# The first loads of a hybrid decoder layer: their order, pieces and buffers

## The chip, the core and the metric

The kernel runs on one core of one Trainium2 chip. The metric is the device time of one execution in microseconds, as the median of several runs. All tensors are float32 in memory; the large products run as split products, in which each operand is cut into a high part (a float32r copy) and a low part (what the copy leaves over).

## The reference, cut to what matters

One decoder layer with 256 tokens and a model width of 2048. A normalised input goes through one combined projection, from which three kinds of token mixers read: six retention heads, six mLSTM heads and 32 groups of an S5 state-space model. Their outputs pass an output projection, and a convolutional gated MLP of width 5632 follows.

```
h = rmsnorm(x, norm1_w)
proj = h @ w_in                      # r_q, r_k, r_v, r_g, m_qk, m_v, m_o, m_gates, s_u
x = x + concat(ret_out, mlstm_out, s5_out) @ w_out
h = rmsnorm(x, norm2_w)
x = x + (silu(gate) * val) @ w_down  # val, gate = split(causal_dwconv(h @ w_up))
return rmsnorm(x, final_norm_w)
```

The change concerns only the beginning: the loads of x, of the parameters and of the 512 columns of `w_in` that make `s_u`, the input of the S5 groups (called the u projection here).

## The kernel before

**Products.** A weight tile `wr` (or `s` for the early pairs, from pool `p4`) is loaded from memory, ScalarE copies it to a float32r tile `wh` (line 412, `highs_to`), and VectorE subtracts to get the low part `wl` (line 423, `lows_to`). The activations are split in the same way into tiles of 512 columns: 256 high, 256 low. A high weight times the whole activation tile and a low weight times the high activation give the product. Matmul, VectorE, ScalarE and GpSimd instructions are all issued through helpers, so the profile shows them on lines 236, 184, 194 and 203, and 219.

**The stream of weights.** All weights form one list, `items`, in the order of their use. `loads_to(i)` (line 381) issues the DMAs up to item i, `highs_to` the casts, `lows_to` the subtractions. The u projection is items 0 to 9: the first four (`NS = 4`) hold one K tile of 128 rows with its 512 columns, 256 KB each, and go to `wr` buffers. Items 4 to 9 hold two K tiles each, 512 KB ("pairs"), and go to six of the eight buffers of pool `p4`, one buffer each, so that no load of a pair waits for a buffer. Later items go through four `wr` buffers.

**The front.** ScalarE's queue issues item 0's DMA and then that of the small parameters `pp0` (lines 1174 and 1175). SP's queue issues everything else: line 1202 loops over j = 0 to 9 and issues the x tile or tiles for item j (`load_x`, 128 KB for a K tile) and then item j. TensorE runs nine matmuls on constants meanwhile.

**The loop of the u projection** (line 1255) goes over the ten items. For each it scales the x tiles by the norm's weight into the high part (ScalarE, for K tile 0 VectorE), subtracts for the low part (VectorE, `scalar_tensor_tensor`), calls `lows_to(j)`, inserts a few small VectorE instructions of the S5 parameters (`fill`), calls `loads_to(j + 4)` (line 1273), squares a tile of x for the norm from j = 4 on, and issues the matmuls: for each K tile four with the high weights, then four with the low ones, into the PSUM tiles `acc` (two) and `u` (two). So K tiles 4 and 5 are item 4, tiles 6 and 7 item 5, and so on.

**Order of the work.** Up to the MLP the schedule is written by hand: the program keeps modelled clocks of the engines and of the DMA (`clk`), and `pump()` places pending tasks (evacuations, S5, heads) between the matmul tiles by these clocks. Each engine then runs its instructions in the order in which they were issued. The small loads in `later` (identity, rotary table, S5 matrices) are issued one behind each weight load.

Of the kernel before, what the change touches and what calls it, by code (L numbers as in the profile page):

```python
# [33 lines left out]
NP0 = _PP["n2"][0]  # L34
# [6 lines left out]
def kernel(ctx: ExitStack, tc: tile.TileContext, a: dict, out: bass.AP):  # L41
    nc = tc.nc
    ADD, SUB, MUL, MAX = ALU.add, ALU.subtract, ALU.mult, ALU.max
# [66 lines left out]
    def free(ap):  # L110
        return int(np.prod(ap.shape[1:]))
# [31 lines left out]
    def landed(ap, at):  # L143
        key, lo, hi = span(ap)
        wrote.setdefault(key, []).append((lo, hi, "dma", at))
# [6 lines left out]
    def reuse(tag, ap, bufs):  # L152

        key = ap.tensor.name
        old = slots.setdefault(tag, [])
        if len(old) >= bufs:
            first = min(old, key=last)
            old.remove(first)
            was_read[key] = [(0, 1 << 30) + x[2:] for tab in (wrote, was_read) for x in tab.get(first, ())]
        old.append(key)  # L160
        return ap
# [68 lines left out]
    V, S, G = Vec(), Act(), Pool()  # L230
# [31 lines left out]
    def add(gen, hi=False):  # L262
        (hi_tasks if hi else lo_tasks).append([gen, ("dve", 0.0)])
# [46 lines left out]
    pp0 = const.tile([128, NP0], F32, name="pp0")  # L310
# [23 lines left out]
    NS = 4  # L334
    items += [([a["wu"][:, 512 * i:512 * (i + 1)]], 512) for i in range(NS)]
    add_stream(a["wu"][:, NS * 512:], (KT - NS) * 512)
    NU = len(items)
# [31 lines left out]
    raw, high, split, ready = {}, {}, {}, {}  # L369
# [4 lines left out]
    auto = [False]  # L374

    later, loaded = [], set()

    def have(*tiles):
        return "obj", lambda: all(t.tensor.name in loaded for t in tiles)

    def loads_to(i):
        while nxt[0] <= min(i, len(items) - 1):
            j = nxt[0]
            ap, n = items[j]
            if NS <= j < NU:

                t = s4()
            else:
                t = reuse("wr", wraw.tile([128, CH], F32, tag="wr", name=f"wr{j}"), 4)
            for i, z in enumerate(ap):  # L390
                (nc.sync if j else nc.scalar).dma_start(out=t[:, i * n // len(ap):(i + 1) * n // len(ap)], in_=z)
            if not auto[0]:
                free_at = max([x[3] for x in was_read.get(t.tensor.name, ())], default=0.0)
                clk.dma = max(clk.dma, free_at + 1.3) + n / 703.0
                landed(t, clk.dma + 0.91)
            if later:

                dst, src = later.pop(0)
                nc.sync.dma_start(out=dst, in_=src)
                clk.dma += free(dst) / 703.0  # L400
                landed(dst, clk.dma + 0.91)
                loaded.add(dst.tensor.name)
            raw[j] = t
            nxt[0] += 1

    def highs_to(i):
        while nxt[1] <= min(i, len(items) - 1):
            j = nxt[1]
            loads_to(j)
            n = items[j][1]  # L410
            h = reuse("wh", whi.tile([128, CH], F32R, tag="wh", name=f"wh{j}"), 4)
            S.copy(h[:, :n], raw[j][:, :n])
            high[j] = h
            nxt[1] += 1

    def lows_to(i):
        while nxt[2] <= min(i, len(items) - 1):
            j = nxt[2]
            highs_to(j)
            n = items[j][1]  # L420
            t, h = raw.pop(j), high.pop(j)
            l = reuse("wl", wlo.tile([128, CH], F32R, tag="wl", name=f"wl{j}"), 3)
            V.tensor_tensor(l[:, :n], t[:, :n], h[:, :n], op=SUB)
            split[j] = (h, l)
            ready[j] = clk.dve + 0.26
            nxt[2] += 1
# [323 lines left out]
    def s4():  # L750
        return p4.tile([128, 1024], F32, tag="s4", name=name("s4"))
# [216 lines left out]
    def ret_heads():  # L968
        yield "obj", lambda: len(rqk) == 6 and (1, 1) in rv
        dec, o_sb, sd = [], {}, {}  # L970
        for h in range(6):
            d = s2()
            later.append((d[:, :384], a["decay"][h]))
            dec.append(d)
        yield have(*dec)

        def scores(hp):
            yield "pe", clk.dve
            yield from grab("mis", 2)
            pss = [mis_t(), mis_t()]  # L980
            for lo, hi, kc, q0 in ((0, 256, 0, 0), (256, 384, 1, 128)):
                for e in range(2):
                    r = slice(64 * e, 64 * e + 64)
                    mm(pss[e][:, lo:hi], lhsT=rqk[3 + hp][r, kc * 128:(kc + 1) * 128], rhs=rqk[hp][r, q0:],
                       start=True, stop=True, par=2)
            yield "dve", clk.pe + 0.2
            for e in range(2):
                d = dec[2 * hp + e]
                V.tensor_tensor(d[:, :384], d[:, :384], pss[e][:, :384], op=MUL)
                sd[2 * hp + e] = d  # L990
            room["mis"] += 2

        yield from scores(0)
        yield from scores(1)
        for half in range(2):
            if half:
                yield from scores(2)
            yield "pe", clk.dve + 0.2
            yield from grab("mis", 2)
            po = [mis_t(), mis_t()]  # L1000
            for i in range(3):
                h = half * 3 + i
                w = slice(i * 128, (i + 1) * 128)
                mm(po[0][:, w], lhsT=sd[h][:, 0:128], rhs=rv[0, half][:, w], start=True, stop=True)
                mm(po[1][:, w], lhsT=sd[h][:, 128:256], rhs=rv[0, half][:, w], start=True, stop=False)
                mm(po[1][:, w], lhsT=sd[h][:, 256:384], rhs=rv[1, half][:, w], start=False, stop=True)
            yield "dve", clk.pe
            for t in range(2):
                o = s2()
                S.copy(o[:, :384], po[t][:, :384])  # L1010
                o_sb[t, half] = o
            room["mis"] += 2
        yield "dve", clk.act + 0.1
        yield from head_norm(o_sb, rg, P("rgn"), 0)
# [156 lines left out]
    manual.enter_context(tc.manual_schedule())  # L1171


    loads_to(0)
    nc.scalar.dma_start(out=pp0, in_=a["pp"][:, :NP0])
    nc.gpsimd.memset(onesm, 1.0)

    nc.scalar.activation(tn([128, 1]), onesm[:, 0:1], AF.Square)
# [11 lines left out]
    def load_x(k, n):  # L1190
        c = k // 2
        if xr[c] is None:
            xr[c] = s2()
        w = slice((k % 2) * T, (k % 2 + n) * T)
        nc.sync.dma_start(out=xr[c][:, w], in_=a["x"][c][:, w])
        clk.dma += 0.37 * n
        for i in range(n):
            xat[k + i] = clk.dma + 0.91
        landed(xr[c][:, w], clk.dma + 0.91)

    kts = [[j] if j < NS else [2 * j - NS, 2 * j - NS + 1] for j in range(NU)]
    for j in range(NU):
        load_x(kts[j][0], len(kts[j]))
        loads_to(j)
    add(ret_heads())
    add(gates())
    add(ml_heads())
# [47 lines left out]
    for j, ks in enumerate(kts):  # L1255
        pump(until=max(last(raw[j].tensor.name), xat[ks[-1]]))
        for k in ks:
            d, x = s2(F32R), xr[k // 2][:, (k % 2) * T:(k % 2 + 1) * T]
            if k == 0:
                V.tensor_scalar(d[:, :T], x, P("n1", k), None, op0=MUL)  # L1260
            else:
                S.activation(d[:, :T], x, AF.Copy, scale=P("n1", k))
            xs.append(d)
        fill(j == 0)

        n = 2 if 0 < j < NS else 1
        for k in ks:
            V.scalar_tensor_tensor(xs[k][:, T:], xr[k // 2][:, (k % 2) * T:(k % 2 + 1) * T], P("n1", k),
                                   xs[k][:, :T], op0=MUL, op1=SUB)
            fill(n)  # L1270
        lows_to(j)
        fill(n + (j == 0))
        loads_to(j + 4)
        if j + 4 == NU:
            rot = s2()
            raws = [s2() for _ in range(4)]
            later += [(ident, a["ident"]), (rot, a["rot"])]
            later += [(raws[i], a["s5b" if i < 2 else "s5c"][i % 2]) for i in range(4)]
            later += [(pp1, a["pp"][:, NP0:])]
            st["raws"] = raws  # L1280
        if j >= NU - 6 and len(sqs) < 8:
            square()
            fill(1)
        hl = split.pop(j)
        for i, k in enumerate(ks):
            o = [slice(i * 512 + f * 128, i * 512 + (f + 1) * 128) for f in range(4)]
            for f in range(4):
                mm(ups[f], lhsT=hl[0][:, o[f]], rhs=xs[k], start=(k == 0), stop=False)
            for f in range(4):
                mm(ups[f][:, T:], lhsT=hl[1][:, o[f]], rhs=xs[k][:, :T], start=False, stop=(k == KT - 1))  # L1290
# [179 lines left out]
    for i in range(NFF):  # L1470
# [6 lines left out]
        j, k = 2 * i, 2 * i + 1  # L1477
# [11 lines left out]
    for f in range(14):  # L1489
        t = fm_sum(fm_tile(st_dn[f], gact, NFF))  # L1490
# [186 lines left out]
```

## Time and profile before

| | us |
|---|---|
| median of 3 runs | 1141.56 |
| lowest and highest of them | 1141.35, 1142.52 |
| the profiled execution | 1142.12 |
| its span | 1140.0 |

In the profile, PE is TensorE's matmuls and PEld its weight loads, DVE is VectorE, ACT ScalarE, POOL GpSimd, and SP the engine that only issues DMAs; a "q" behind the name is the engine's queue when it issues. A row of a timeline gives start, duration, engine, line, operation and tiles (out<-in), and in brackets the idle time before it and what ended it. A row of a DMA view gives the count of issues, the size of one and the median microseconds from issue to landing. A row of the waits gives the total, the number of waits and the longest. In a row of stages the figures are the busy time of PE, PEld, DVE, ACT and POOL, TensorE's granted clock, the DMA's share and GB/s.

### The profile page before, as it was taken

What the parts mean: (1) busy time and instruction counts of PE and PEld (TensorE: products, weight loads), DVE (VectorE), ACT (ScalarE), POOL (GpSimd) and SP (SyncE); (2) the same over time, 40 slices, a digit from 0 to 9 for tenths busy, and PEclk for the clock granted to TensorE, in tenths of its full rate; (3) what the DMA queues carried; (4) which work ended last, traced back from release to release, by engine and by line L of the source; (5) the groups of instructions that cost most, each with busy time, mean ns of one, the idle gap of its engine ahead of it and who ended that gap; (6) DMA issues with size and microseconds to landing.
All of it is one profiled execution on the core that took longest, in us unless ns stands there. A gap on an engine that the chain in (4) does not pass through costs nothing.

```text
span 1140.0 us, 18148 instructions
## 1 busy us (share of the span) xinstructions
PE 1128.1 (99%) x6660; PEld 1009.4 (89%) x6660; DVE 875.5 (77%) x1532; ACT 629.6 (55%) x996; POOL 84.8 (7%) x170
## 2 busy tenths in 40 slices
PE   9999999999999999999999999999999999999997
PEld 8899888998988888888888888888888888888897
DVE  8899989998989977777777777777777545544454
ACT  7665567345656765555555555555555444444442
POOL 7506050022000000000000000000000000000000
PEclk9999999999999999999999999999999999999999
DMA  8657555555676655555556555555655566666663
GB/s 317 213 168 242 171 162 160 153 159 151 189 244 210 201 186 185 188 191 192 191 191 192 184 187 187 191 191 190 193 191 188 177 197 183 188 187 192 194 189 108
DMA packets 68933, 215.87 MB, mean 189 GB/s; under 512 B 7782, under 2 KB 11116, under 8 KB 68844
## 3 DMA queue, kind: packets, MB, share of 16 engines
q1 hardware_dynamic: 68556, 214.41, 59.4%
q8 instruction: 52, 0.85, 0.3%
q14 instruction: 37, 0.30, 0.1%
q10 hardware_dynamic: 288, 0.31, 0.1%
HBM read 212.58 MB, written 2.10 MB: 188 GB/s over the span
## 4 chain that ended last, share of the span: by engine, by line
PE 95%; DVE 1%; ACT 1%; POOL 1%; DMA 1%; issue 0%; SPq 0%; DVEq 0%; ACTq 0%; POOLq 0%
PE acc L236 90%; PE mis L236 3%; PE wo L236 1%; POOL t L219 1%; DVE s L184 1%; ACT s L203 1%; PE u L236 1%; DMA s<-in_wu_dram 1%; DVE wl L184 1%; PE mis L240 0%; ACT wh L194 0%; DMA wr<-in_wu_dram 0%; DVE t L184 0%; ACT L203 0%; POOL tp L219 0%
## 5 line engine op out<-in xcount | busy, mean ns | idle before, releaser
L194 ACT CAST wh<-wr 128x1024 fp32r<-128x1024 f32 (+3 forms) x411 | 408.0, 995 | 417.7 <-PE acc L236 263.3
L236 PE MATMUL acc<-s,wh 128*128 128x512 f32 x2372 | 579.2, 392 | 1.0 <-ACT wh L194 0.6
L184 DVE TENSOR_TENSOR wl<-wr,wh 128x1024 fp32r<-128x1024 f32 (+3 forms) x411 | 462.8, 1150 | 148.1 <-PE acc L236 94.9
L236 PEld LDWEIGHTS acc<-s,wh 128*128 128x128 f32 x2372 | 432.6, 188 | 82.8 <-ACT wh L194 0.8
L236 PEld LDWEIGHTS acc<-s,wl 128*128 128x128 f32 x2372 | 310.7, 191 | 16.2 <-DVE wl L184 0.5
L236 PE MATMUL acc<-s,wl 128*128 128x256 f32 x2372 | 317.9, 283 | 0.1
L184 DVE TENSOR_TENSOR s<-s,s 128x256 f32<-128x256 f32 (+5 forms) x271 | 127.4, 487 | 45.5 <-ACT s L203 41.8
L236 PE MATMUL acc<-wh,s 128*128 128x384 f32 (+2 forms) x632 | 157.6, 329 | 0.0
L184 DVE SCALAR_TENSOR_TENSOR s<-s,pp,s 128x255 f32<-128x255 f32 (+3 forms) x244 | 116.7, 479 | 8.5 <-ACT s L203 5.3
L236 PEld LDWEIGHTS acc<-wh,s 128*128 128x128 f32 x632 | 112.1, 189 | 2.3 <-issue 1.5
L236 PE MATMUL acc<-wl,s 128*128 128x384 f32 (+2 forms) x316 | 103.3, 327 | 1.0 <-DVE wl L184 1.0
L203 ACT ACTIVATE s<-s,pp 128x256 f32<-128x256 f32 (+1 forms) x145 | 81.8, 568 | 15.4 <-DVE s L184 14.6
L184 DVE TENSOR_TENSOR s<-acc,s 128x256 f32<-128x256 f32 x138 | 57.6, 421 | 38.9 <-ACT s L194 35.8
L219 POOL TENSOR_TENSOR t<-t,neg_half 128x2 f32<-128x2 f32 (+1 forms) x4 | 2.5, 635 | 870.0 <-DVE t L184 870.0
L236 PEld LDWEIGHTS acc<-wl,s 128*128 128x128 f32 x316 | 59.6, 189 | 2.0 <-DVE wl L184 1.9
L203 ACT ACTIVATE s<-s 128x256 f32<-128x256 f32 (+2 forms) x105 | 45.0, 429 | 28.8 <-DVE s L184 28.7
L194 ACT COPY s<-acc 128x256 f32<-128x256 f32 (+1 forms) x142 | 52.0, 369 | 3.0 <-PE acc L236 2.8
L236 PE MATMUL acc<-g,wh 128*128 128x512 f32 x196 | 49.5, 392 | 0.0
L184 DVE TENSOR_TENSOR s<-s,rbc 128x256 f32<-128x256 f32 x106 | 44.7, 425 | 6.1 <-ACT rbc L194 3.1
L236 PEld LDWEIGHTS acc<-g,wh 128*128 128x128 f32 x196 | 35.8, 188 | 6.9
L236 PE MATMUL mis<-s,s 128*32 128x256 f32 (+6 forms) x216 | 25.8, 340 | 0.6 <-DVE s L184 0.6
L236 PEld LDWEIGHTS acc<-g,wl 128*128 128x128 f32 x196 | 25.4, 191 | 1.1
(105 smaller groups left out, 471.0 us busy)
## 6 DMA issues: line engine op xcount, KB each, us to landing
wr<-in_wup_dram SPq DMA_DIRECT2D x176, 512.0 KB, 4.8
wr<-in_wdn_dram SPq DMA_DIRECT2D x70, 512.0 KB, 4.2
wr<-in_wtm_dram SPq DMA_DIRECT2D x56, 384.0 KB, 3.3
wr<-in_wfm_dram SPq DMA_DIRECT2D x36, 512.0 KB, 5.0
wr<-in_wout_dram SPq DMA_DIRECT2D x16, 512.0 KB, 4.5
wr<-in_wdt_dram SPq DMA_DIRECT2D x11, 512.0 KB, 3.7
wr<-in_wout_dram SPq DMA_DIRECT2D x20, 256.0 KB, 4.2
s<-in_x_dram SPq DMA_DIRECT2D x14, 256.0 KB, 6.8
```

Of the source, the lines that this page charges most:

```text
L184: return real(o, *args, **kw)
L194: return nc.scalar.copy(o, i)
L203: return nc.scalar.activation(o, i, fn, **kw)
L219: return real(o, *args, **kw)
L236: nc.tensor.matmul(o, lhsT=lhsT, rhs=rhs, start=start, stop=stop)
```

## The change

- The parameters' DMA is issued before that of item 0, both still on ScalarE's queue.
- The cast of item 0 and both the cast and the subtraction of item 4 (the first pair) are made in two halves of its columns. Item 0's subtraction stays whole.
- Item 4 is loaded in two DMAs of one K tile each, and its two x tiles one by one, in the order x, weights, x, weights.
- The pairs use three `p4` buffers in turn instead of six. Before the loop only items 0 to 6 are issued; pair j + 3 (with its x tiles) is issued in the loop after `lows_to(j)`. The later items are issued from j = 7 on with `loads_to(j + 4)`.

```diff
@@ loads_to
             if NS <= j < NU:
-                t = s4()
+                if len(early_w) < 3:
+                    early_w.append(s4())
+                t = early_w[(j - NS) % 3]
             else:
                 t = reuse("wr", wraw.tile([128, CH], F32, tag="wr", name=f"wr{j}"), 4)
+            if j == NS:
+                ap = [ap[0][:, :512], ap[0][:, 512:]]
             for i, z in enumerate(ap):
+                if j == NS:
+                    load_x(kts[j][i], 1)
                 (nc.sync if j else nc.scalar).dma_start(out=t[:, i * n // len(ap):(i + 1) * n // len(ap)], in_=z)
@@
+    def halves(j, n):
+        return (slice(0, n // 2), slice(n // 2, n)) if j in (0, NS) else (slice(0, n),)
@@ highs_to
-            S.copy(h[:, :n], raw[j][:, :n])
+            for w in halves(j, n):
+                S.copy(h[:, w], raw[j][:, w])
@@ lows_to
-            V.tensor_tensor(l[:, :n], t[:, :n], h[:, :n], op=SUB)
+            for w in halves(j, n) if j else (slice(0, n),):
+                V.tensor_tensor(l[:, w], t[:, w], h[:, w], op=SUB)
@@ the front
+    nc.scalar.dma_start(out=pp0, in_=a["pp"][:, :NP0])
     loads_to(0)
-    nc.scalar.dma_start(out=pp0, in_=a["pp"][:, :NP0])
@@
-    for j in range(NU):
-        load_x(kts[j][0], len(kts[j]))
+    def load(j):
+        if j < NU and j != NS:
+            load_x(kts[j][0], len(kts[j]))
         loads_to(j)
+    for j in range(NS + 3):
+        load(j)
@@ the loop
-        loads_to(j + 4)
+        if NS <= j < NU - 3:
+            load(j + 3)
+        elif j >= NU - 3:
+            loads_to(j + 4)
```

More of the change, by code (lines that the diff above doesn't have):

```diff
@@ L376 @@
     later, loaded = [], set()
+    early_w = []
     def have(*tiles):
```

## The prediction

> **What bounds the kernel now.** I read the page's busy shares first, then the chain of waits over the first 60 us, then the engines' timelines there, and last who keeps TensorE waiting after 30 us.
>
> ```profile
> span 1140.0 us, 18148 instructions
> PE 1128.1 (99%) x6660; PEld 1009.4 (89%) x6660; DVE 875.5 (77%) x1532; ACT 629.6 (55%) x996; POOL 84.8 (7%) x170
> ```
>
> TensorE is busy for 1128.1 of 1140.0 us. No edit touches a matmul, so all that this change can move is a part of the 11.9 us in which TensorE stands, or runs behind its data. The chain of waits (start, us, what) shows which part lies in the front:
>
> ```profile
> 0.71 3.25 DMA wr<-in_wu_dram
> ...
> 4.83 6.62 DMA s<-in_wu_dram
> ...
> 11.55 1.06 ACT wh L194
> 12.63 1.24 DVE wl L184
> ...
> 30.08 5.59 PE acc L236 x32
> ```
>
> The chain runs through the DMA of the first pair of K tiles (4.83, landed at 11.45), the cast of the whole pair on ScalarE and its subtraction on VectorE. Only from 13.91 on is it TensorE that follows TensorE, to 30.08, where the u projection ends, and beyond. So TensorE as it stands at 13.91 is what the change can bring forward. TensorE's own timeline (start, us, what, in brackets the idle time before it):
>
> ```profile
> 5.63 1.19 PE L236 MATMUL acc<-s,wh 128*128 128x512 f32 x2 [0.45 <-DVE t L184]
> ...
> 12.65 0.73 PE L236 MATMUL acc<-s,wh 128*128 128x512 f32 x2 [0.56 <-ACT wh L194]
> 13.22 0.63 PE L236 MATMUL u<-s,wh 128*128 128x512 f32 x2
> 13.91 0.50 PE L236 MATMUL acc<-s,wl 128*128 128x256 f32 x2
> ...
> 16.82 0.40 PE L236 MATMUL acc<-s,wl 128*128 128x256 f32 x2
> 19.62 0.40 PE L236 MATMUL acc<-s,wl 128*128 128x256 f32 x2
> 22.43 0.40 PE L236 MATMUL acc<-s,wl 128*128 128x256 f32 x2
> ```
>
> The first real matmul starts at 5.63; TensorE idles 0.56 us before the first pair's high part (12.65) and a little before its low part (13.91). The last three rows are the low parts that open K tiles 6, 8 and 10; they are 2.8 us apart, two K tiles of 1.40. VectorE stands behind all of this:
>
> ```profile
> 4.54 0.17 DVE L184 TENSOR_SCALAR t<-pp 128x4 f32<-128x4 f32 x1 [4.54 <-DMA pp<-in_pp_dram]
> 5.00 0.48 DVE L184 SCALAR_TENSOR_TENSOR s<-s,pp,s 128x256 fp32r<-128x256 f32 x1
> 5.51 0.68 DVE L184 TENSOR_TENSOR wl<-wr,wh 128x512 fp32r<-128x512 f32 x1
> 6.11 0.18 DVE L184 TENSOR_SCALAR t<-t 128x16 f32<-128x16 f32 x1
> 12.63 1.23 DVE L184 TENSOR_TENSOR wl<-s,wh 128x1024 fp32r<-128x1024 f32 x1 [0.47 <-ACT wh L194]
> 13.77 0.40 DVE L184 SCALAR_TENSOR_TENSOR t<-t,t 128x16 f32<-128x16 f32 x2
> 15.07 1.22 DVE L184 TENSOR_TENSOR wl<-s,wh 128x1024 fp32r<-128x1024 f32 x1
> 17.96 1.21 DVE L184 TENSOR_TENSOR wl<-s,wh 128x1024 fp32r<-128x1024 f32 x1
> 20.80 1.22 DVE L184 TENSOR_TENSOR wl<-s,wh 128x1024 fp32r<-128x1024 f32 x1
> 25.90 1.21 DVE L184 TENSOR_TENSOR wl<-s,wh 128x1024 fp32r<-128x1024 f32 x1
> ```
>
> VectorE waits for the parameters until 4.54 and then has one wait that counts, 0.47 us at 12.63. The subtractions of the pairs end at 16.29, 19.17 and 22.02, and TensorE takes their results at 16.82, 19.62 and 22.43: only 0.53, 0.45 and 0.41 us later. This is the point on which my sum turns: **VectorE is nearly as late as TensorE**, so closing TensorE's gaps gains only what VectorE can follow, plus that margin.
>
> **The change, part by part.** *Parameters first.* Both DMAs go out on ScalarE's queue; the parameters are issued first now, the weights second.
>
> ```profile
> 0.71 0.41 ACTq L391 DMA_DIRECT2D wr<-in_wu_dram  x1
> 1.15 0.46 ACTq L1175 DMA_DIRECT2D pp<-in_pp_dram  x1
> pp<-in_pp_dram ACTq DMA_DIRECT2D x1, 42.0 KB, 3.4
> 3.99 0.62 ACT L194 CAST wh<-wr 128x512 fp32r<-128x512 f32 x1 [0.85 <-DMA wr<-in_wu_dram]
> L194 ACT CAST s<-s 128x256 fp32r<-128x256 f32 x34 | 13.9, 408 | 7.4 <-DVE s L184 7.3
> ```
>
> The parameters' 3.4 us from issue to landing, started 0.44 earlier, puts them at about 4.1; then VectorE's scaling, filler and low part run 0.44 earlier, and TensorE's first inputs are there at 5.48 − 0.44 = 5.04. The weights, issued 0.46 us later, land at about 3.97 + 0.48 = 4.45. Cast in halves of 256 columns (the last row's shape, a mean of 408 ns; two of them some 0.1 more than the 0.62 of one), the first half is ready at 4.87 and the second at about 5.2. So the first matmul starts near 5.1, half a microsecond earlier, and the first subtraction, which is not halved, at 5.24 instead of 5.51. That is 0.27 us for VectorE; between 4.54 and 12.1 us its instructions follow each other without a wait of weight, so it keeps them to the first pair. Bounds: nothing if the weights lose 0.75 us instead of 0.48; 0.44 if they lose under 0.3. I take 0.27. ScalarE's next casts wait for their own weights in any case, which hides its later start; without that cover it would be 0.6 us.
>
> *The first pair one by one.* Its 768 KB now come as x, half the weights, x, half the weights: two DMAs more on SP's queue. The row of the cast before it and that of its own, and the two issues of w4 and the pair after:
>
> ```profile
> 8.12 0.62 ACT L194 CAST wh<-wr 128x512 fp32r<-128x512 f32 x1 [0.31 <-DMA wr<-in_wu_dram]
> 11.55 1.05 ACT L194 CAST wh<-s 128x1024 fp32r<-128x1024 f32 x1 [1.05 <-DMA s<-in_wu_dram]
> 4.83 0.44 SPq L391 DMA_DIRECT2D s<-in_wu_dram  x1
> ```
>
> Weights 3 landed at 8.1 and the pair at 11.45, so 768 KB took 3.35 us. Laid out in the new order this gives x at 8.7, half the weights at 9.8, x at 10.35, the rest at 11.45. ScalarE scales both x tiles before it casts: the second ends at 10.86, the first half is cast by about 11.5 and the other by 12.1, against 12.60 for the whole. The two added issues cost about 0.9 us on SP's queue (0.44 each), and pairs 5 and 6 are queued behind them; those DMAs land over 6 us after issue, so they are bounded by bytes and not by the issue, and I cost them at nothing (0.9 us at most if that cover were gone).
>
> Now VectorE, whose filler ended at 12.63 − 0.47 = 12.16, is free at 12.16 − 0.27 = 11.89, later than the half cast at 11.5: its wait is gone. The first half is subtracted by 11.89 + 0.69 = 12.58, and TensorE opens its low part at 12.62 instead of 13.91, a gain of 1.29. A half costs VectorE 0.60 us (5.51 to 6.11, next start), the whole 1.14 (12.63 to 13.77); so two halves cost 0.06 to 0.08 more, and VectorE goes on at 13.11 where it went on at 13.77: 0.66 earlier. That fixes the rest. The next subtractions end at 15.63, 18.51 and 21.36; with 0.04 us to TensorE its low parts open at 15.67, 18.55 and 21.40, against 16.82, 19.62 and 22.43: gains of 1.15, 1.07 and 1.03. **What is left at 30.08 is 1.0 us**: 0.66 of VectorE and 0.37 of margin, used up. What is late next is VectorE.
>
> [...]
>
> *Three buffers in turn.* Pairs 7, 8 and 9 now load into the buffers of pairs 4, 5 and 6, when those are cast and subtracted. SP issues in order, so x of pair 8, pair 9 and the first weights of the next projection queue behind each such wait.
>
> ```profile
> 8.67 0.74 SPq L391 DMA_DIRECT2D s<-in_wu_dram  x1
> 13.41 0.33 SPq L391 DMA_DIRECT2D s<-in_wu_dram  x1
> s<-in_wu_dram SPq DMA_DIRECT2D x1, 512.0 KB, 8.5
> wr<-in_wup_dram SPq DMA_DIRECT2D x176, 512.0 KB, 4.8
> ```
>
> Weights 7 move from 8.67 to 13.2 (after the second half's subtraction, 12.50 + 0.69), weights 8 to 15.7, weights 9 from 13.41 to 18.6, and the next projection's weights, right behind, to about 19.0. Subtraction 7 is due at 20.14, and its cast takes 1.05, so weights 7 have 5.9 us to land; weights 9, with subtraction 9 due at 25.24, have 5.6. In the crowded front the same 512 KB took 8.5 us, later in the kernel the median is 4.8. By 13 us the queue holds only pairs 5 and 6, so I take the lower end and cost this at nothing, with 1 us to spare. The next projection's weights have 7 us and more.
>
> *Sum.* The profiled execution took 1142.12 us with a span of 1140.0; 1.0 less gives 1141.1, span 1139.0. The median of the runs, 1141.56, is 0.56 below the profiled one, so I forecast 1140.5 for it.
>
> **Does the gain reach the end?** Who keeps TensorE waiting from 30 us to the end:
>
> ```profile
> PE mis L240 <- DVE s L184: 2.9, 2, 2.1
> PE acc L236 <- DVE wl L184: 1.0, 3, 0.5
> PE mis L236 <- DVE s L184: 0.6, 1, 0.6
> 60.00:90.00 30.00, 30.00 (x184) 28.88 (x183) 29.47 (x89) 19.42 (x38) 4.49 (x8) 1.00 0.60 173
> ```
>
> Total 4.5 us, 2.1 of it one wait at the end. The other 2.4 are five short waits for VectorE. It is 98% busy in stretches like the last row (third figure, 29.47 of 30 us), but the data that it works on come from TensorE, so I expect both to shift together.
>
> **Rivals.** *The three buffers starve the pairs* (slower). If weights 7 still take 8.5 us, they land at 21.7, are cast by 22.8, and subtraction 7 ends at 24.0 instead of 22.02; TensorE opens K tile 10's low part at 24.06, not 22.43, 1.6 us later than before: 1143.2. The point from which it decides: a landing over 5.9 us. Against it: fewer bytes are queued, and 4.8 is the rule elsewhere. Chance 0.04.
>
> *The gain is swallowed* by VectorE between 60 and 280 us, where it is full: if its work there is set by something that does not shift (GpSimd's chain of parameters, a DMA), the five waits grow by 1.0 us and the time stays at 1141.6. For it: 98%. Against it: TensorE waits only 2.4 us there. Chance 0.14.
>
> *The order changes.* The program lays out the later work by modelled clocks, and the edits move modelled landings and casts, so evacuations may fall elsewhere between the tiles. The five waits of 2.4 us may double (−1.0 + 2.4: 1143.0) or go (1138.1). Nothing in the profile tells which; 0.06 and 0.06.
>
> *More than my sum.* Were VectorE no limit, TensorE would run K tiles 0 to 3 from 5.1 and all else without a gap: 0.5 at the start, 0.56, and the 0.2 before the low part, and up to 0.7 more from the slow first tile, 1.9 at most: 1139.7. Against it is VectorE's margin. Chance 0.10.
>
> *The halves do nothing*, because TensorE and VectorE wait for the whole tile: the pair would be ready when its second half is, at 12.1, still half a microsecond before 12.60; subtraction starts at 12.13 instead of 11.89, leaving 0.8: it lies inside the forecast.
>
> **How the numbers follow.** Forecast 0.60 (1139.9 to 1141.2), swallowed 0.14, more 0.10, order 0.06 each way, starving 0.04. 0.2% is 2.3 us, about what a measurement of this kernel can tell from no change; the forecast's 1.0 is under half of it. Over 2.3 us faster: the order's good side and some of "more", 0.10 in all. Over 2.3 us slower: the tails of the bad order and of starving, 0.05. The rest, 0.85, is within. The range, 1139.2 to 1142.3, takes in the forecast, the swallowed gain and "more", and leaves out the order's two ends and starving, 0.16.
>
> **What would show it.** Right: first matmul near 5.1, VectorE's wait at the first pair's subtraction gone, the first pair's low part at about 12.6, K tile 10's low part at about 21.4, the projection after u from about 29.05; weights 7 issued near 13.2 and landed before 19. Wrong: a wait of a cast for weights 7, 8 or 9 with VectorE behind it; the u projection ending before 28.6 or after 29.6; or waits for VectorE after 30 us that sum to another figure than 4.5.

## The result, and the profile after

| | median | runs | profiled execution's span |
|---|---|---|---|
| before | 1141.57 us | 1141.35 to 1142.52 (5) | 1140.0 us |
| after | 1150.14 us | 1148.63 to 1150.92 (5) | 1148.1 us |

The ratio is 1.0074, with a 95% interval of 1.0062 to 1.0085: 8.6 us slower, where 1.0 us faster was forecast and 1142.3 was the upper end.

The busy shares of the changed kernel, from its page:

```profile
span 1148.1 us, 18148 instructions
PE 1132.1 (99%) x6660; PEld 1011.0 (88%) x6660; DVE 877.7 (76%) x1533; ACT 629.0 (55%) x998; POOL 78.3 (7%) x170
```

TensorE stands for 16.0 us where it stood for 11.9, and is busy for 4.0 us more with the same 6660 matmuls. So in this pair of profiles about half of the 8.1 us is idle time and half is slower matmuls. The front is not where they arise. Its rows in the changed kernel, from the chain of waits (the first) and TensorE's timeline:

```profile
29.78 5.59 PE acc L236 x32
```
```profile
5.64 0.74 PE L236 MATMUL acc<-s,wh 128*128 128x512 f32 x2 [0.45 <-ACT wh L194]
...
13.20 0.51 PE L236 MATMUL acc<-s,wl 128*128 128x256 f32 x2
...
16.18 0.50 PE L236 MATMUL acc<-s,wl 128*128 128x256 f32 x2
...
19.23 0.50 PE L236 MATMUL acc<-s,wl 128*128 128x256 f32 x2
...
22.13 0.41 PE L236 MATMUL acc<-s,wl 128*128 128x256 f32 x2
```

The u projection ends 0.3 us earlier, not later (29.78 against 30.08). The loss lies behind it: the waits of TensorE after 30 us, four of them in its timeline between 250 and 350 us, and five stages, of which the first is the kernel before and the others are the changed kernel:

```profile
PE acc L236 <- DVE s L184: 3.3, 3, 2.4
PE mis L240 <- DVE s L184: 4.6, 3, 2.1
PE mis L236 <- DVE s L184: 1.2, 2, 1.1
```
```profile
257.95 0.45 PE L240 MATMUL mis<-ident,s 128*128 128x128 f32 x2 [1.98 <-DVE s L184]
...
311.64 0.49 PE L236 MATMUL acc<-s,wh 128*128 128x512 f32 x1 [0.46 <-DVE s L184]
314.55 0.80 PE L236 MATMUL acc<-s,wh 128*128 128x512 f32 x1 [2.41 <-DVE s L184]
...
348.96 0.50 PE L236 MATMUL mis<-s,wh 128*128 128x512 f32 x1 [1.06 <-DVE s L184]
```
```profile
300.00:330.00 30.00, 30.00 (x174) 26.39 (x173) 29.93 (x53) 19.11 (x27) 0.00 (x0) 1.00 0.64 203
```
```profile
255.00:260.00 5.00, 2.87 (x24) 1.53 (x22) 3.76 (x6) 5.00 (x11) 0.00 (x0) 0.82 0.28 77
...
310.00:315.00 5.00, 2.01 (x7) 1.20 (x8) 3.29 (x12) 4.31 (x8) 0.00 (x0) 0.78 0.18 67
315.00:320.00 5.00, 5.00 (x18) 4.28 (x18) 4.15 (x8) 2.58 (x5) 0.00 (x0) 0.54 0.37 108
320.00:325.00 5.00, 5.00 (x29) 4.30 (x28) 4.46 (x7) 3.72 (x6) 0.00 (x0) 1.00 0.65 200
```

The waits sum to 9.1 us (before: 4.5); both sums hold the same wait of 2.06 us at the very end, so what stands between is 7.0 us against 2.4, and some of these waits are long. In the stages the third figure from the end is TensorE's granted clock. It is 1.00 in every 30 us stage of the kernel before up to 450 us; here, after the wait of 2.41 us, it is 0.54 for the next five microseconds, in which TensorE gets through 18 matmuls instead of about 30. So slow matmuls came on top of this wait, which lies in a stage of five (310 to 315) with 2.01 us of matmuls. Near 258 two waits of 1.98 and 0.15 us go with a clock of 0.82 from 255 to 260.

Why are VectorE's results late? GpSimd's timeline shows one thing that moved, first before, then after:

```profile
10.33 0.63 POOL L219 TENSOR_TENSOR t<-pp,t 128x16 f32<-128x16 f32 x1 [1.36 <-DVE t L184]
...
39.39 0.74 POOL L219 TENSOR_TENSOR t<-t,neg_half 128x2 f32<-128x2 f32 x1
...
45.92 0.12 POOL L714 MEMSET s<- 128x16 f32 x1
```
```profile
37.91 1.62 POOL L219 TENSOR_TENSOR t<-t,neg_half 128x2 f32<-128x2 f32 x1 [30.66 <-DVE t L184]
39.50 1.01 POOL L219 TENSOR_TENSOR t<-pp,t 128x16 f32<-128x16 f32 x1
...
68.64 0.13 POOL L729 MEMSET s<- 128x16 f32 x1
```

The `t<-pp,t` row is the first step of the S5 parameters' chain (`s5_params`), and the memset follows its last. Before, the chain started at 10.33 and the first norm's power (`t<-t,neg_half`, in `rsqrt_`) was put between its steps. After, the power stands ahead of the chain. The rows show GpSimd running its queue in order: the power's input comes only at 37.9, so GpSimd idles for 30.66 us and the chain ends 23 us later. Nobody edited that: the order was laid out anew by the modelled clocks. Between 60 and 90 us VectorE then has less to do (25.09 us busy, before 29.47). That this work comes later, where TensorE waits for it, was my reading; no row shows it, and two experiments below show that it is not the whole cause. The stage:

```profile
60.00:90.00 30.00, 30.00 (x184) 28.91 (x183) 25.09 (x64) 17.75 (x35) 12.51 (x37) 1.00 0.57 163
```

Why it turned can be read in the code and in the program's own clocks (modelled microseconds, no times of the chip). `pump()` takes a low-priority step only while VectorE's modelled clock is under TensorE's plus 0.35. At the first `pump()` behind the u projection that was 32.02 against 32.44: the chain was issued, by a margin of 0.42. With the three buffers the modelled landings of pairs 7 to 9 wait for their buffers and push back those of the next projection's weights. ScalarE's modelled clock there is 30.83 instead of 28.21, VectorE's is 32.90 against TensorE's 32.51, and the chain has to wait for a later `pump()`, behind the power.

### The profile page after: what moved, and what is told of

Its sections match the earlier page's. It is cut to its first block, busy times and chain, and to the rows that moved or that the text cites. A ratio compares the mean times of both kernels' runs of the same rounds, so it can differ in the third digit from the quotient of the medians.

```text
span 1148.1 us, 18148 instructions
## 1 busy us (share of the span) xinstructions
PE 1132.1 (99%) x6660; PEld 1011.0 (88%) x6660; DVE 877.7 (76%) x1533; ACT 629.0 (55%) x998; POOL 78.3 (7%) x170
## 4 chain that ended last, share of the span: by engine, by line
PE 96%; DVE 2%; POOL 1%; ACT 1%; DMA 0%; issue 0%; DVEq 0%; ACTq 0%; POOLq 0%
PE acc L236 91%; PE mis L236 3%; DVE s L184 1%; PE u L236 1%; PE wo L236 1%; POOL t L219 1%; PE mis L240 0%; ACT s L203 0%; DMA wr<-in_wu_dram 0%; DVE wl L184 0%; ACT L203 0%; ACT wh L194 0%; ACT s L194 0%; POOL tp L219 0%; DVE t L184 0%
## 5 line engine op out<-in xcount | busy, mean ns | idle before, releaser
L194 ACT CAST wh<-wr 128x1024 fp32r<-128x1024 f32 (+4 forms) x412 | 407.8, 992 | 423.1 <-PE acc L236 269.3
L184 DVE TENSOR_TENSOR wl<-wr,wh 128x1024 fp32r<-128x1024 f32 (+3 forms) x411 | 462.9, 1150 | 150.8 <-PE acc L236 93.9
```

The lines of the kernel that those rows point to most:

```text
L184: return real(o, *args, **kw)
L194: return nc.scalar.copy(o, i)
```

## The experiments

Theory 1: the order of the later work lost the time; the loads gained a little. Theory 2, the rival: the later loads and SP's blocked queue lost it.

**The new loads in the old order.** The DMAs, halves and buffers of the change are issued as they stand, but `clk` is advanced as in the kernel before. Two places of the edit; what is `held` is issued in the loop:

```diff
+            if NS + 3 <= j < NU:
+                held.append((j, t, ap, n))
+            else:
+                issue(j, t, ap, n)
...
-                free_at = max([x[3] for x in was_read.get(t.tensor.name, ())], default=0.0)
+                free_at = 0.0 if NS <= j < NU else max([x[3] for x in was_read.get(t.tensor.name, ())], default=0.0)
```

> All four parts of the change as they stand (parameters first, halves, first pair one by one, three buffers), but the modelled clocks that lay out the later work are kept as they were before, so every engine has the order of before. Theory 1 (the order of the later work lost the time, the loads did not): 1141.3 us, since the u projection ends 0.3 us earlier in the changed kernel (29.78 against 30.08). Theory 2 (the later loads and SP's blocked queue lost it): 1149 to 1151.

Measured: 1141.87 us, ratio 1.0001 (0.9993 to 1.0010). The loads cost nothing that can be measured, and gain nothing that can.

**The old loads in the new order**, the reverse: `clk` is advanced as in the changed kernel, everything issued in the front is as before. Two places of the edit: each pair has its own buffer, loaded ahead of the loop, and `key` is for the clock alone.

```diff
-                t = early_w[(j - NS) % 3]
+                t = early_w[j]
...
+                key = (early_w[j - 3] if NS + 3 <= j < NU else t).tensor.name
```

> The reverse: loads, casts and buffers of before, but the modelled clocks, and so the order of the later work, of the changed kernel. Theory 1: 1150.4 us, that of the changed kernel plus the 0.3 us of the front. Theory 2: 1141.6.

Measured: 1150.61 us, 1.0075 (1.0061 to 1.0089). The whole loss is back without one changed load, and so are the waits, one by one (with one of 0.28 us more); its timeline:

```profile
259.36 0.41 PE L240 MATMUL mis<-ident,s 128*128 128x128 f32 x2 [1.98 <-DVE s L184]
259.96 1.07 PE L236 MATMUL mis<-s,s 128*32 128x256 f32 x16 [0.19 <-DVE s L184]
...
314.58 0.79 PE L236 MATMUL acc<-s,wh 128*128 128x512 f32 x1 [2.41 <-DVE s L184]
315.18 0.84 PE L236 MATMUL acc<-s,wl 128*128 128x256 f32 x3
...
320.45 0.52 PE L236 MATMUL acc<-s,wl 128*128 128x256 f32 x3
```

Theory 2 falls; theory 1 holds. The split into idle time and slow matmuls is not fixed. Behind the wait of 2.41 us the matmuls were slow as in the changed kernel (three with low weights took 0.84 us in both, and 0.52 at 320). Behind the wait of 1.98 us sixteen took 1.07 us here and 1.94 in the changed kernel, at the same span of 1148.1 us; the changed kernel's row:

```profile
258.54 1.94 PE L236 MATMUL mis<-s,s 128*32 128x256 f32 x16 [0.15 <-DVE s L184]
```

**The three buffers alone**, on the kernel before: the hunks on `early_w`, the loop ahead and `load(j + 3)`, nothing else.

> Only the three buffers in turn, on the kernel before. Theory 1: this part alone moves the modelled landings of the next projection's weights, and so turns the order: 1149 to 1151 us with GpSimd's chain ending near 69 us. If another part turns it: 1141.6.

Measured: 1151.24 us, 1.0079 (1.0064 to 1.0095); GpSimd's chain ends at 71.33. This part is enough to turn the order.

**One modelled number**, on the kernel before:

```diff
-                landed(t, clk.dma + 0.91)
+                landed(t, clk.dma + 0.91 + (2.6 if NU <= j < NU + 4 else 0.0))
```

> The kernel before with not one instruction, buffer or transfer changed: only the modelled landing of the next projection's first four weight loads is set 2.6 us later (the shift that the three buffers give it), so the order of the later work comes out anew. Theory 1: 1148 to 1151 us, GpSimd's chain ending near 69 us. If the transfers themselves matter: 1141.6.

Measured: 1148.18 us, 1.0053 (1.0038 to 1.0069), the power ahead of the chain and the chain's end at 68.45. With every instruction, buffer and transfer as before, that shows the link from modelled landing to order to time.

**The S5 chain put back ahead**, in the changed kernel:

```diff
+    early = [t for t in lo_tasks if t[0].__name__ == "s5_params"][0]
+    for _ in range(11):
+        step(lo_tasks, early)
     def squares():
```

> The changed kernel with one thing put back: the first eleven steps of the S5 parameters are issued on GpSimd's queue ahead of the norm's power, as before. If that one chain (46 us finished before, 69 us after) carries the loss: 1141 to 1143 us. If the rest of the order counts as much, since everything behind it is laid out anew: about 1146. Theory 2: 1149 to 1151.

Measured: 1147.63 us, 1.0051 (1.0037 to 1.0064). The chain ends at 48.08, near its old place (45.92), but only 2.5 of the 8.6 us come back; a new wait of 4.58 us stands at 266.77:

```profile
266.77 0.85 PE L240 MATMUL mis<-ident,s 128*128 128x128 f32 x2 [4.58 <-DVE s L184]
```

So the chain is not the whole cause: theory 1 holds for the order as a whole, and blaming this one chain was too narrow.

**All but the three buffers.** Parameters first, halves and one by one, with six buffers and all loads ahead of the loop.

> The changed kernel with six buffers and all loads ahead of the loop again, so parameters first, halves and one by one alone, with the order that the modelled clocks then give. GpSimd's chain stays ahead of the norm. If only that chain's place counts: 1141.3 us (the front's 0.3). If any shift of the modelled clocks, here 0.1 us from the halves, is enough to lay the later work out worse: 1143 to 1146.

Measured: 1149.92 us, 1.0068 (1.0054 to 1.0082): as slow as the whole change, and above both figures that I had expected, with GpSimd's chain in its old place (its end at 45.47). Its waits are others:

```profile
266.24 0.85 PE L240 MATMUL mis<-ident,s 128*128 128x128 f32 x2 [4.30 <-DVE s L184]
...
316.44 0.80 PE L236 MATMUL acc<-s,wh 128*128 128x512 f32 x1 [2.85 <-DVE s L184]
```

So the other parts spoil the order too, by a different way. In the modelled clocks they add only the fixed part of the second half of a split instruction.

**A modelled 68 ns**, and **a modelled 150 ns**, on the kernel before, with no instruction touched (0.068 in the first, 0.15 in the second):

```diff
             V.tensor_tensor(l[:, :n], t[:, :n], h[:, :n], op=SUB)
+            if j == NS:
+                clk.dve += 0.068
```

> The kernel before with no instruction, transfer or buffer changed: the program's modelled clock of VectorE is set 68 ns later at the first pair's subtraction (what the halves add to it), and the later order follows from that. The run without the three buffers lost 8 us with GpSimd's chain in its old place, waiting 4.3 us at 266. If the halves' modelled cost is what laid that order out: 1149 to 1151 us with the same waits near 266 and 316. If the halves' transfers or real cost did it: 1141.7.

> The same with 150 ns instead of 68. If the loss grows with the size of the shift: over 1150 us. If the order turns at a threshold, either way, and the size means nothing: 1141 to 1143.

Measured: 1149.52 us (1.0059, 1.0041 to 1.0077), and 1137.95 us (0.9963, 0.9949 to 0.9978). The first has the waits of the run before it to a hundredth or so; the second has none between the front and the end. Waits after 30 us, 68 ns and then 150 ns:

```profile
PE mis L240 <- DVE s L184: 6.4, 2, 4.3
PE acc L236 <- DVE s L184: 2.9, 1, 2.9
```
```profile
PE mis L240 <- DVE s L184: 2.1, 1, 2.1
```

I had expected 1141 to 1143 or more than 1150 of the larger shift; it is 3.9 us *faster* than the kernel before. A larger shift did not lose more; the order comes out well or badly.

**Can the front be had on top?** Two variants in the old order: the first weights ahead of the parameters again; and the parameters on SP's queue ahead of x, with the norm's power issued ahead of two squarings of the chain.

> As the run with the order of before and all four parts, but the first weights issued ahead of the parameters again. In the changed kernel the weights landed at 5.16, 1.2 us later than before, and VectorE's first subtraction at 5.93 instead of 5.51. With the weights first: subtraction at 5.5, the first pair's low part near 12.9, end of the u projection near 29.3. But the norm's power then still starts at 39.4 or later on GpSimd, so TensorE waits for it at 41.7: 1141.4 us, not 1140.7. If GpSimd's queue is no limit there: 1140.8.

> The order of before, all parts of the front, with two differences: the parameters on SP's queue ahead of the first x tile (so the first weights stay first on ScalarE's), and the norm's power on GpSimd ahead of two squarings of the S5 chain. The u projection should end near 29.0 and the transposes of the norm no longer wait at 41.7 but follow TensorE at 41.0: 1140.6 us. If the gain is lost elsewhere down the way: 1141.6.

Measured: 1142.10 us (1.0003, 0.9994 to 1.0011) and 1141.43 us (0.9997, 0.9989 to 1.0006): neither can be told from no change. Their u projections ended earlier than before, at about 29.3 where TensorE's timeline of the kernel before has 29.92, but not at 29.0. The wait for the norm's power that the first expectation put at 41.7 is not in that run's profile; the run with all four parts has it, 0.25 us at 41.74.

The same two, in the order of the 150 ns run:

> The order of the 150 ns run (1137.95 us) with the front of this change, only the first weights ahead of the parameters again. The front brought 0.5 to 0.8 us by 41 us in such runs; with no wait of TensorE behind it until the end, it should arrive: 1137.3 us. If the front's gain is lost on the way as in the order of before: 1137.9.

> The same with the parameters on SP's queue and the norm's power ahead of the S5 chain: 1137.3 us; 1137.9 if the front's gain is lost.

Measured: 1138.33 us (0.9969, 0.9956 to 0.9981) and 1138.22 us (0.9969, 0.9956 to 0.9981). All three runs in that order beat the kernel before by 3.4 to 3.9 us (differences of medians), and the front adds nothing to it that shows: both runs lie above the 1137.3 and the 1137.9 expected. In the first of the two, part of the front's gain is lost as the expectation for the old order had it, in a wait for the norm's power on GpSimd:

```profile
42.03 0.43 PE L240 MATMUL mis<-ident,t 128*128 128x128 f32 x2 [0.46 <-POOL t L219]
```

## Why the prediction was wrong, point by point

**The step that failed** is the part "Does the gain reach the end?": "I expect both to shift together". It took the later order as given, and so put the cost of a new order at nothing in the sum. The rival "the order changes" named the mechanism, but at 0.06 for the bad side, and it priced it at a doubling of the waits that stood there, 2.4 us. Measured, the waits after 30 us grew by 4.6 us (4.5 to 9.1), and slower matmuls, for which the price had no term, added 4.0; the first 30 us, with 1.48 us of idle TensorE instead of 2.04, gave back 0.6. Neither the chance nor the price follows from what was known. The code shows a threshold, and the modelled landings of pairs 7 to 9 and of all that follows move by the very edit I was costing; it could have been asked what that does at the first `pump()`. And the waits of an order that came out well say nothing of those of another: the runs with an order laid out anew took 1137.95 to 1151.24 us, and in the changed kernel a wait of 2.41 us was followed by five microseconds at a granted clock of 0.54 on top.

**Starving by the three buffers** did not happen, as forecast. Weights 7 went out at 13.77 (forecast 13.2), and landed in 4.1 us, weights 9 in 4.7; I had taken 4.8 against an upper bound of 8.5. ScalarE's casts of pairs 7, 8 and 9 did wait for their weights, 0.18, 0.25 and 1.00 us, but each was done 0.7 us or more before VectorE's subtraction began. The issues of weights 7 and 9:

```profile
s<-in_wu_dram SPq DMA_DIRECT2D x1, 512.0 KB, 4.1
...
s<-in_wu_dram SPq DMA_DIRECT2D x1, 512.0 KB, 4.7
```

**Parameters first** was mis-sized. They landed after 2.5 us instead of my 3.4, but the weights, second now, took 4.0 from issue and their cast began at 5.18, not 4.45:

```profile
pp<-in_pp_dram ACTq DMA_DIRECT2D x1, 42.0 KB, 2.5
...
wr<-in_wu_dram ACTq DMA_DIRECT2D x1, 256.0 KB, 4.0
```
```profile
5.18 0.71 ACT L194 CAST wh<-wr 128x256 fp32r<-128x256 f32 x2 [2.05 <-DMA wr<-in_wu_dram]
```

That is beyond the 0.75 us at which I had put the gain for VectorE at nothing: its first subtraction came at 5.93 instead of 5.51, and the first matmul at 5.64 instead of 5.63, not near 5.1. In four profiled runs with this front (one of them with six buffers) the cast began at 4.32, 4.67, 4.92 and 5.18, and the u projection's successor at 28.87, 29.23, 29.46 and 29.61. The 28.87 is the forecast 1.0 us (before: 29.92 in the same timeline), and it belongs to the cast at 4.32, near the forecast 4.45. But four runs of the unchanged front had 29.34, 29.36, 30.24 and 30.45 there: the front's own scatter, 1.1 us, is larger than its gain, some 0.6 us in the mean (four runs against these four and the kernel before). The prediction had no term for that scatter.

**The first pair** went as worked out in kind, but not in size: VectorE's wait is gone, its half subtraction and the low part follow, and the low parts of K tiles 4, 6, 8 and 10 came 0.7, 0.6, 0.4 and 0.3 us earlier, where 1.3, 1.15, 1.07 and 1.03 had been forecast. VectorE itself began the first pair's subtraction only 0.17 us earlier (12.46 against 12.63) and the third pair's no earlier (17.95 against 17.96), where 0.74 and 0.66 had been forecast. What TensorE gained at the third pair, 0.4 us, is the margin that the prediction had named. **The halves** do something: the low part at 13.20 opens before the second half is subtracted (12.46 and 1.28 for both). They cost VectorE 1.21 us from start to next start, where the whole cost 1.14: 0.07 more, as forecast.

## What to carry to other kernels

Where a program lays out its work by modelled clocks, an edit is two changes: the instructions that it touches, and the order of everything behind it. Time the two apart, by issuing the new instructions under the old clocks, before judging the edit. And try a few meaningless shifts of those clocks first: here 68 ns and 150 ns of modelled time were worth +7.6 and −3.9 us (differences of medians), many times what the edit to the front could bring.

## What the runs showed of the hardware

- A waiting instruction held all that stood behind it on GpSimd's queue: a power of 128 x 2 elements held GpSimd for 30.66 us and, behind it, the chain, which ended at 68.64 instead of 45.92.
- In the changed kernel TensorE's granted clock was 0.54 from 315 to 320 us, behind a wait of 2.41 us, and 1.00 in the next 5. Sixteen matmuls behind a wait of 1.98 us took 1.94 us there and 1.07 in the run of the old loads in the new order. Of the 8.1 us between the two profiled spans, 4.0 are matmuls that took longer.
- A 256 KB transfer issued behind one of 42 KB on the same queue was ready for its reader between 4.32 and 5.18 us in four runs; issued first, between 3.87 and 4.17 in ten others.

What stays open: which of the moved steps cause the wait near 266 us in the runs without the late chain, and what in the 150 ns order makes it good. The runs show that it is the order, not which part of it.
